# Four low halves back on GpSimd and three loads behind named pieces, in the first mixer of a two-layer block

## The chip, the cores and the metric

The kernel runs on one core of a Trainium2 chip. A core has a matrix engine (TensorE, "PE" in the profile; its weight loads are listed as PEld), a vector engine (VectorE, DVE), a scalar engine (ScalarE, ACT), GpSimd (POOL) and a queue that issues the loads (SyncE, SP). Each works through its own list of instructions in order and waits for the others by semaphores. SBUF is the on-chip memory, PSUM the banks that TensorE writes. The metric is the device time of one execution in microseconds (us); lower is better. Times quoted as "median" are over several executions; every row of the profile is from one profiled execution.

## The reference, cut to what matters

Two layers over 256 tokens of width 2048, all in float32. Layer 0 mixes by a convolution and by averages over windows ("pool"), layer 1 by a short gated convolution; each is followed by a gated feed-forward layer. Only the first mixer is touched by the change:

```python
def conv_pool_mixer(x, norm_g, w_in, conv_w, conv_b, ln_g, ln_b, w_pool, pool_scale, w_out):
    h = rms_norm(x, norm_g)
    u = h @ w_in                                   # 2048 -> 3 * 1024
    a = u[..., :D_CONV] * jax.nn.sigmoid(u[..., D_CONV:2 * D_CONV])
    a = causal_depthwise_conv(a, conv_w) + conv_b  # 31 taps
    a = jax.nn.silu(layer_norm(a, ln_g, ln_b))
    p = multiscale_pool(u[..., 2 * D_CONV:], w_pool, pool_scale)   # windows 2, 4, 8, 16, then 256 x 256 per group
    return jnp.concatenate([a, p], axis=-1) @ w_out

def reference(...):
    ...
            h = h + conv_pool_mixer(...)
        ...
        h = h + swiglu(rms_norm(h, ffn_norm[i]), w_gate[i], w_up[i], w_down[i])
    return rms_norm(h, final_norm)
```

## The kernel before, in words

**Weights and products.** Activations are kept with features on the 128 partitions and the 256 tokens along the row. All weights lie in one tensor (`wall`) in the order of their use, cut into blocks of 128 x 128. `fetch(u)` (L207) loads one unit of up to 16 blocks, 1024 KB, into one of four buffers named `w`; the first nine units are smaller and carry the first chunks of the input as well. A unit is used in pieces of 8 blocks (of 4 in the first units). For each piece, `prepare` (L222) calls `halves_of` (L213): ScalarE rounds the piece to the matrix engine's format (`hi`, L218), and another engine subtracts (`lo = w - hi`, L219). `hi` and `lo` have five buffers each, and some pieces use a spare pair. A block's product is three matmuls (L311 to L313): hi times the rounded activations, hi times their remainder, lo times the rounded activations. So TensorE needs a piece's low half before it can finish the first block of that piece. `advance` (L251) prepares up to four pieces ahead of the block in use in the first mixer, and fetches one unit beyond that.

**Who subtracts.** VectorE makes the low halves, except for the pieces whose first block number lies in `POOL_SPLIT` (72 to 519): these go to GpSimd. `relief` is a list to which each pool group adds one entry when it has been written out (L681); the next such piece that is prepared takes the entry and goes to VectorE. There are four pool groups, so four pieces go to VectorE: those that start at blocks 128, 224, 328 and 360.

**The first mixer's order on TensorE.** The first 64 blocks are four chunks side by side (two of the convolution, each with its gate), then come the two chunks of pool group 3 (64 to 95), and then the rest by `M0_ORDER`: a convolution chunk and its gate are 32 blocks, a pool group's two chunks 32, a group's own 256 x 256 matrix 4. The convolutions end at block 391, the groups 1 and 0 are 392 to 399, the projection of the pool half is 400 to 527, and the projection of the convolution half follows.

**What runs beside it.** `gated` multiplies a convolution chunk by its gate (VectorE L477, L633, L634). `tap` then convolves two chunks with 31 taps on VectorE, accumulating in PSUM (L536, L538), with half of the products made by ScalarE (L533) and added by VectorE (L540). `pooled` evicts a group's chunks on VectorE (L668), sums over the window in doubling steps on GpSimd (L674), corrects the first tokens (L676) and subtracts the input (L677); ScalarE rounds the result (L679) and VectorE writes its remainder (L680, two operands from SBUF). The layer norm's first part (`ln_mean`, `ln_center`) runs from VectorE, GpSimd and four matmuls of TensorE (L568); its last part (`ln_last`) starts with VectorE's L547 after the last tap, passes TensorE (L595, L587, L419) and ends with ScalarE's L624 and L626, from which the convolution half's projection reads.

**The input norm.** The square sum per token is taken from token rows: `square_rows(j)` (L495) loads 128 tokens by 2048 (1024 KB) into the one buffer `rows` and squares them on ScalarE (L498). From the two sums come the factors per token, spread to all partitions by a diagonal (VectorE L409, with the identity that lies at the end of `vec`) and a product (TensorE L419); VectorE copies the result (L461) and the first chunks can be evicted.

**What sets the order.** The context is opened with `schedule_with_timeline_sim=True`: the order of instructions on each engine is fixed when the program is built, from the order of the program text, its dependencies and an estimated timeline. `tc.issue_after(ins)` adds that what is issued inside stands behind `ins` on the same queue. `behind_weights(dst, src)` (L485) queues a load behind the latest `fetch` of the text so far (`state_pe["dma"]`).

Of the kernel before, what the change touches and what calls it, by code (L numbers as in the profile page):

```python
# [20 lines left out]
NC = D // P  # L21
# [101 lines left out]
def x_of(u):  # L123
    return X_CHUNKS[u] if u < len(X_CHUNKS) else 0
# [63 lines left out]
def block_kernel(ctx: ExitStack, tc: tile.TileContext, xT: bass.AP, xtok: bass.AP, vec: bass.AP, wall: bass.AP, out: bass.AP):  # L188
    nc = tc.nc
# [9 lines left out]
    banks = {}  # L199
    loaded, ready = {}, {}  # L200
    cursor = {"token": 0, "piece": 0, "P": 0, "S": 0}
    relief = []

    def new_acc(shape=(P, T), name="acc"):
        return banks["acc"].tile(list(shape), F32, name=name, tag="acc")

    def fetch(u):  # L207
        if u < len(UNITS) and u not in loaded:
            n, off = UNITS[u][3], UNIT_AT[u] * P * P
            loaded[u] = w = wst.tile([P, 16 * P], F32, name="w")  # L210
            state_pe["dma"] = nc.sync.dma_start(w[:, : n * P], wall[off : off + n * P * P].rearrange("(p f) -> p f", p=P)).ins

    def halves_of(src, at, n, engine, spare=False):  # L213
        if spare:
            hi, lo = (banks["spare"].tile([P, W_ROOM], F32R, name=x)[:, SPARE_AT : SPARE_AT + n] for x in ("hi", "lo"))
        else:
            hi, lo = (whl.tile([P, W_ROOM], F32R, name=x)[:, at : at + n] for x in ("hi", "lo"))
        state_pe["hi"] = nc.scalar.copy(hi, src).ins  # L218
        engine.tensor_tensor(out=lo, in0=src, in1=hi, op=ALU.subtract)  # L219
        return hi, lo  # L220

    def prepare(i):  # L222
        if i >= len(PIECES):
            return
        _, u, key, what = PIECES[i]
        if key in ready:
            return
        fetch(u)
        w = loaded[u]
        if key[0] == "P":  # L230
            o, n = what
            if x_of(u):
                for j in range((o - 2 * x_of(u)) // 4, (o - 2 * x_of(u) + n) // 4):
                    norm.scale(sum(X_CHUNKS[:u]) + j, w[:, j * T : (j + 1) * T])
            engine = nc.vector
            if key[1] in POOL_SPLIT:
                if relief:
                    relief.pop()
                else:
                    engine = nc.gpsimd  # L240
            ready[key] = halves_of(w[:, o * P : (o + n) * P], 0, n * P, engine, key[1] in SPARE and i % 6 == 5)
            return
        lo, n = ((0, 512), (1024, 1024), (0, 1024), (1024, 1024))[what]
        ready[key] = halves_of(w[:, lo : lo + n], S_SHIFT, n, nc.vector)
        if what == 0:
            nc.vector.tensor_tensor(out=w[:, :1024], in0=w[:, 512:1536], in1=w[:, :1024], op=ALU.subtract)
        if what == 1:
            nc.vector.tensor_tensor(out=w[:, 1024:1536], in0=w[:, 1024:1536], in1=w[:, :512], op=ALU.subtract)
            nc.vector.tensor_tensor(out=w[:, 1536:], in0=w[:, 1024:1536], in1=w[:, 1536:], op=ALU.subtract)
# [13 lines left out]
    def next_block():  # L263
        assert KINDS[cursor["token"]] == 0
        advance()
        b = cursor["P"]
        cursor["P"] = b + 1
        at = max(k[1] for k in ready if k[0] == "P" and k[1] <= b)
        hi, lo = ready[("P", at)]
        for k in [k for k in ready if k[0] == "P" and k[1] < at]:  # L270
            ready.pop(k)
        o = (b - at) * P
        return hi[:, o : o + P], lo[:, o : o + P]
# [22 lines left out]
    def tick():  # L296
        for name, q in queues.items():
            credit[name] = credit[name] + 1.0 if q else 0.0
            while q and credit[name] >= PACE[q[0][0]]:
                cost, step = q.popleft()  # L300
                credit[name] -= PACE[cost]
                step()
# [7 lines left out]
    def product(acc, hi, lo, x, first, last, part=False):  # L310
        nc.tensor.matmul(acc, hi, x[:, :T], start=first, stop=False, skip_group_check=part)  # L311
        nc.tensor.matmul(acc, hi, x[:, T:], start=False, stop=False, skip_group_check=part)  # L312
        state_pe["last"] = nc.tensor.matmul(acc, lo, x[:, :T], start=False, stop=last, skip_group_check=part).ins  # L313

    def matmul_chunks(xs, ks, n=1, behind=None, accs=None):


        accs = accs or [new_acc() for _ in range(n)]
        for i, k in enumerate(ks):
            first, last = i == 0, i == len(ks) - 1  # L320
            x = xs[k] if isinstance(xs, dict) else xs[:, k, :]
            for acc in accs:
                hi, lo = next_block()
                product(acc, hi, lo, x, first, last)
                tick()
            if behind is not None:
                behind(k)
        return accs
# [14 lines left out]
    v = const.tile([P, NVEC], F32, name="v")  # L343
# [138 lines left out]
    xs = norm.xs  # L482
    nc.sync.dma_start(v[:, :NC], vec[:, :NC])

    def behind_weights(dst, src):  # L485
        with tc.issue_after(state_pe["dma"]):
            nc.sync.dma_start(dst, src)

    def loads_behind(k):
        if k == 3:  # L490
            behind_weights(v[:, NC:], vec[:, NC:])
        if k == 4:
            square_rows(1)

    def square_rows(j):  # L495
        rows = x0_pool.tile([P, D + 64], F32, name="rows")[:, :D]
        behind_weights(rows, xtok[:, j, :])
        nc.scalar.activation(rows, rows, AF.Square, accum_out=rowsq[:, j : j + 1])  # L498

    x0 = ctx.enter_context(ExitStack())  # L500
    x0_pool = x0.enter_context(tc.tile_pool(name="x0", bufs=1))
    rowsq = const.tile([P, 2], F32, name="rowsq")
    for u in range(6):
        fetch(u)
    square_rows(0)
    every = range(NC)
    with tc.tile_pool(name="ps0", bufs=5, space=PSUM) as ps0, tc.tile_pool(name="m0", bufs=1) as m0, tc.tile_pool(name="ps_side", bufs=2, space=PSUM) as ps_side:
        phase[0] = m0, None, 2
# [120 lines left out]
        def gated(acc_v, acc_g, c):  # L629
# [7 lines left out]
            if c % 2:  # L637
                convolve(c - 1)

        first = matmul_chunks(xs, every, n=4, behind=loads_behind)  # L640
        rest = norm.rstd(rowsq, behind=True)
        for at in (0, NC // 2):
            behind_weights(h[:, at : at + NC // 2, :], xT[:, at : at + NC // 2, :])
# [15 lines left out]
        def pooled(g, accs=None):  # L659


            w = WINDOWS[g]
            xp = m0.tile([P, 2, pp + T], F32, name="xp", bufs=2)
            nc.gpsimd.memset(xp[:, :, :pp], 0.0)
            less = m0.tile([P, 2, T], F32, name="pm", bufs=2)
            for j in range(2):
                acc = accs[j] if accs else matmul_chunks(xs, every)[0]
                nc.vector.tensor_tensor(out=xp[:, j, pp:], in0=acc, in1=r, op=ALU.mult)  # L668
                nc.scalar.activation(less[:, j, :], xp[:, j, pp:], AF.Copy, scale=-float(w))
            cur, step = xp, 1  # L670
            while step < w:
                nxt = m0.tile([P, 2, pp + T], F32, name="sw", bufs=2)
                lo = pp - (w - 2 * step)
                nc.gpsimd.tensor_tensor(out=nxt[:, :, lo:], in0=cur[:, :, lo:], in1=cur[:, :, lo - step : pp + T - step], op=ALU.add)  # L674
                cur, step = nxt, 2 * step
            nc.gpsimd.tensor_tensor(out=cur[:, :, pp : pp + w - 1], in0=cur[:, :, pp : pp + w - 1], in1=corr[:, g, :, : w - 1], op=ALU.mult)  # L676
            nc.gpsimd.tensor_tensor(out=less, in0=cur[:, :, pp:], in1=less, op=ALU.add)  # L677
            dst = cat[:, 2 * g : 2 * g + 2, :]
            nc.scalar.activation(dst[:, :, :T], less, AF.Copy, scale=1.0 / w)  # L679
            nc.vector.scalar_tensor_tensor(out=dst[:, :, T:], in0=less, scalar=1.0 / w, in1=dst[:, :, :T], op0=ALU.mult, op1=ALU.subtract)  # L680
            relief.append(1)  # L681

        room = moving(x0_pool.tile([P, D + 64], F32R, name="room", tag="rows"), Y_AT, 4)
        mixed = {}
        for kind, i in M0_ORDER:
            if kind == "pool":
                pooled(i, early)
                early = None
                continue
            if kind == "group":  # L690
                for j in range(2):
                    (acc,) = matmul_chunks(cat, range(2 * i, 2 * i + 2))
                    mixed[2 * i + j] = xs[:, 2 * i + j, :] if i < 2 else room[:, 2 * i + j - 4, :]
                    split(mixed[2 * i + j], acc, col("pool_scale", 2 * i + j))
                continue
            (acc_v,) = matmul_chunks(xs, every)
            (acc_g,) = matmul_chunks(xs, every)
            gated(acc_v, acc_g, i)
# [315 lines left out]
```

## Time and profile before

| | us |
|---|---|
| median of 3 executions | 2008.69 (2006.31 to 2010.91) |
| the profiled execution | 2007.14 |
| its span, first to last instruction | 2004.9 |

| busy | us of the span | share |
|---|---|---|
| TensorE | 1984.6 | 99% |
| VectorE | 1706.8 | 85% |
| ScalarE | 1158.7 | 58% |
| GpSimd | 203.1 | 10% |

How to read the rows: in a timeline a row is start, duration, engine, line, operation, output tile <- input tiles, shapes and the number of merged instructions; a bracket at its end is the idle time before it and what ended it. A row of grouped instructions gives the count, then after the first bar the busy time (us) and the mean of one (ns), and after the second bar the idle time before them. A row of a stage begins with the stage's bounds and length, followed by the busy time and count of TensorE, its weight loads, VectorE, ScalarE and GpSimd, the granted clock of TensorE (1.00 is full), the share of DMA time, and GB/s. A row of one line's instructions gives the shortest, median and longest duration in ns, and the first and last start.

### The profile page before, as it was taken

How to read it: one execution, taken by the hardware profiler on the slowest of the kernel's cores; microseconds unless marked ns; L12 is line 12 of the kernel's file. 1: busy time of each engine (PE TensorE's matmuls, PEld its weight loads, DVE VectorE, ACT ScalarE, POOL GpSimd, SP SyncE). 2: the span in 40 equal slices, each digit the busy share in tenths (PEclk: the TensorE clock that was granted, in tenths of full speed). 3: DMA queues.
4: the chain of work that ended last, by engine and by line, in shares of the span. 5: the costliest groups of instructions: out<-in, count | busy, mean ns of one | idle time of the engine just before them, and what ended most of it. 6: DMA issues, size and time to landing. Idle time of an engine off the chain costs nothing.

```text
span 2004.9 us, 41548 instructions
## 1 busy us (share of the span) xinstructions
PE 1984.6 (99%) x17346; PEld 1981.3 (99%) x17346; DVE 1706.8 (85%) x2302; ACT 1158.7 (58%) x1527; POOL 203.1 (10%) x184
## 2 busy tenths in 40 slices
PE   9999999999999999999999999999999999999998
PEld 9999999999999999999999999999999999999997
DVE  6998888999988999989666666788999988999985
ACT  7788675655555555556444444565555555555554
POOL 3996200000000000002000001100000000000002
PEclk9999999999999999999999999999999999999999
DMA  9555445545555555546555555454554555555552
GB/s 362 189 190 211 148 171 208 202 185 207 206 196 205 190 210 199 203 191 229 189 193 198 199 190 191 167 211 171 208 210 190 210 211 209 200 201 190 190 228 88
DMA packets 55772, 398.27 MB, mean 199 GB/s; under 512 B 6304, under 2 KB 6560, under 8 KB 8352
## 3 DMA queue, kind: packets, MB, share of 16 engines
q1 hardware_dynamic: 55584, 395.61, 52.9%
q8 instruction: 136, 2.23, 0.4%
q14 instruction: 52, 0.43, 0.1%
HBM read 393.49 MB, written 2.10 MB: 197 GB/s over the span
## 4 chain that ended last, share of the span: by engine, by line
PE 92%; DVE 5%; ACT 1%; DMA 1%; issue 0%; DVEq 0%; SPq 0%; POOL 0%; ACTq 0%; POOLq 0%
PE acc L312 22%; PE acc L311 22%; PE acc L313 22%; PE s L796 8%; PE s L797 8%; PE s L795 8%; DVE side L538 2%; DVE side L540 1%; DVE lo L219 1%; PE acc L751 1%; DMA rows<-in_xtok 0%; PE s L311 0%; PE s L312 0%; PE s L313 0%; ACT hi L218 0%
## 5 line engine op out<-in xcount | busy, mean ns | idle before, releaser
L218 ACT CAST hi<-w 128x1024 fp32r<-128x1024 f32 (+1 forms) x933 | 922.4, 1004 | 742.9 <-PE acc L312 347.3
L219 DVE TENSOR_TENSOR lo<-w,hi 128x1024 fp32r<-128x1024 f32 (+1 forms) x881 | 1014.1, 1174 | 184.4 <-ACT hi L218 172.2
L311 PE MATMUL acc<-xs,hi 128*128 128x256 f32 x2416 | 663.0, 276 | 3.0 <-DVE gate L477 2.6
L312 PE MATMUL acc<-xs,hi 128*128 128x256 f32 x2416 | 662.4, 276 | 0.0
L313 PE MATMUL acc<-xs,lo 128*128 128x256 f32 x2416 | 660.1, 276 | 1.0 <-POOL lo L219 1.0
L311 PEld LDWEIGHTS acc<-xs,hi 128*128 128x128 f32 x2416 | 452.9, 188 | 4.1 <-ACT prod L533 1.7
L312 PEld LDWEIGHTS acc<-xs,hi 128*128 128x128 f32 x2416 | 452.6, 188 | 0.0
L313 PEld LDWEIGHTS acc<-xs,lo 128*128 128x128 f32 x2416 | 450.8, 188 | 1.5 <-POOL lo L219 1.2
L312 PE MATMUL acc<-y,hi 128*128 128x256 f32 x1408 | 387.7, 276 | 0.0
L311 PE MATMUL acc<-y,hi 128*128 128x256 f32 x1408 | 387.6, 276 | 0.0
L313 PE MATMUL acc<-y,lo 128*128 128x256 f32 x1408 | 383.5, 276 | 0.0
L312 PEld LDWEIGHTS acc<-y,hi 128*128 128x128 f32 x1408 | 264.4, 188 | 0.0
L311 PEld LDWEIGHTS acc<-y,hi 128*128 128x128 f32 x1408 | 264.2, 188 | 0.0
L313 PEld LDWEIGHTS acc<-y,lo 128*128 128x128 f32 x1408 | 262.2, 188 | 0.0
L795 PE MATMUL s<-hi,sf 128*128 128x256 f32 x768 | 210.9, 277 | 0.0
L796 PE MATMUL s<-hi,sf 128*128 128x256 f32 x768 | 210.0, 275 | 0.0
L450 POOL TENSOR_TENSOR sumsq<-sumsq,sq 128x256 f32<-128x256 f32 x56 | 53.2, 951 | 1526.7 <-ACT sq L448 1526.3
L797 PE MATMUL s<-lo,sf 128*128 128x256 f32 x768 | 206.5, 276 | 0.0
L797 PE MATMUL s<-lo,xs 128*128 128x256 f32 x576 | 159.0, 276 | 0.0
L795 PE MATMUL s<-hi,xs 128*128 128x256 f32 x576 | 159.0, 276 | 0.0
L796 PE MATMUL s<-hi,xs 128*128 128x256 f32 x576 | 158.8, 276 | 0.0
L795 PEld LDWEIGHTS s<-hi,sf 128*128 128x128 f32 x768 | 144.3, 188 | 0.0
(193 smaller groups left out, 2665.1 us busy)
## 6 DMA issues: line engine op xcount, KB each, us to landing
w<-in_wall SPq DMA_DIRECT2D x365, 1024.0 KB, 4.9
w<-in_wall SPq DMA_DIRECT2D x7, 768.0 KB, 7.3
rows<-in_xtok SPq DMA_DIRECT2D x2, 1024.0 KB, 8.6
h<-in_xT SPq DMA_DIRECT2D x2, 1024.0 KB, 11.8
out<-res SPq DMA_DIRECT2D x2, 512.0 KB, 2.7
w<-in_wall SPq DMA_DIRECT2D x2, 384.0 KB, 4.1
out<-res SPq DMA_DIRECT2D x2, 384.0 KB, 2.7
v<-in_vec SPq DMA_DIRECT2D x1, 260.0 KB, 7.6
```

The lines of the kernel that those rows point to most:

```text
L218: state_pe["hi"] = nc.scalar.copy(hi, src).ins
L219: engine.tensor_tensor(out=lo, in0=src, in1=hi, op=ALU.subtract)
L311: nc.tensor.matmul(acc, hi, x[:, :T], start=first, stop=False, skip_group_check=part)
L312: nc.tensor.matmul(acc, hi, x[:, T:], start=False, stop=False, skip_group_check=part)
L313: state_pe["last"] = nc.tensor.matmul(acc, lo, x[:, :T], start=False, stop=last, skip_group_check=part).ins
L450: nc.gpsimd.tensor_tensor(out=self.sums[0], in0=self.sums[0], in1=sq, op=ALU.add)
L538: nc.vector.scalar_tensor_tensor(out=dst, in0=src, scalar=wt, in1=dst, op0=ALU.mult, op1=ALU.add)
L540: nc.vector.tensor_tensor(out=side, in0=side, in1=prods.pop((c, k)), op=ALU.add)
L751: nc.tensor.transpose(bank[:, c, t * P : (t + 1) * P], part[:, c * P : (c + 1) * P], identity)
L795: nc.tensor.matmul(acc, xh, hi, start=first, stop=False, skip_group_check=True)
L796: nc.tensor.matmul(acc, xl, hi, start=False, stop=False, skip_group_check=True)
L797: nc.tensor.matmul(acc, xh, lo, start=False, stop=last, skip_group_check=True)
```

## The change

Two things are done. First, `relief` is removed: every piece in `POOL_SPLIT` has its low half made by GpSimd, the four at blocks 128, 224, 328 and 360 among them. Second, three loads are attached to pieces of the weights by number: `fetch` looks up its unit in `load_behind` and runs what it finds right behind that unit's load. The first token rows stand behind unit 5 as before. The rest of `vec` (the vectors, with the identity) stands behind unit 6; before, it was issued at the end of the fourth input chunk of the first products. The second token rows stand behind unit 8; before, they were issued at the end of the fifth input chunk, behind the latest load of that moment (unit 7).

```diff
     cursor = {"token": 0, "piece": 0, "P": 0, "S": 0}
-    relief = []
...
+    load_behind = {}
 
     def fetch(u):
         if u < len(UNITS) and u not in loaded:
...
+            if u in load_behind:
+                load_behind[u]()
...
             if key[1] in POOL_SPLIT:
-                if relief:
-                    relief.pop()
-                else:
-                    engine = nc.gpsimd
+                engine = nc.gpsimd
...
-    def loads_behind(k):
-        if k == 3:
-            behind_weights(v[:, NC:], vec[:, NC:])
-        if k == 4:
-            square_rows(1)
-
...
+    load_behind[5] = partial(square_rows, 0)
+    load_behind[6] = lambda: behind_weights(v[:, NC:], vec[:, NC:])
+    load_behind[8] = partial(square_rows, 1)
     for u in range(6):
         fetch(u)
-    square_rows(0)
...
-        first = matmul_chunks(xs, every, n=4, behind=loads_behind)
+        first = matmul_chunks(xs, every, n=4)
...
-            relief.append(1)
```

## The prediction

> **What bounds the kernel now.** I read the page first, then the busy time by stages, TensorE's waits, and the timelines of VectorE and GpSimd.
>
> ```profile
> span 2004.9 us, 41548 instructions
> PE 1984.6 (99%) x17346; PEld 1981.3 (99%) x17346; DVE 1706.8 (85%) x2302; ACT 1158.7 (58%) x1527; POOL 203.1 (10%) x184
> ...
> 52.00:138.00 86.00, 85.80 (x756) 85.80 (x757) 82.20 (x138) 65.25 (x119) 81.50 (x46) 1.00 0.55 197
> 138.00:158.00 20.00, 15.62 (x128) 14.96 (x127) 17.06 (x32) 18.72 (x35) 20.00 (x11) 1.00 0.53 194
> ```
>
> TensorE is busy 1984.6 of 2004.9 us, so a change outside its work can win back only its 20 us of waits. The stage rows (busy time of TensorE, its weight load, VectorE, ScalarE, GpSimd, each with its count) show that the first mixer is different from the average: GpSimd, 10% busy over the span, is busy 81.50 of 86.00 us there and 20.00 of 20.00 in the next stage. VectorE is nearly as full. TensorE waits little before 138 us, then 4.4 us in 20. Its waits, one row each, in time order (the bracket holds the wait and its releaser):
>
> ```profile
> 52.20 0.39 PE L313 MATMUL acc<-xs,lo 128*128 128x256 f32 x1 [0.98 <-POOL lo L219]
> 140.54 0.36 PE L311 MATMUL acc<-xs,hi 128*128 128x256 f32 x1 [1.57 <-DVE gate L477]
> 147.73 1.13 PE L568 MATMUL st<-total,ones 128*128 128x256 f32 x4 [2.25 <-DVE total L552]
> 149.76 0.28 PE L313 MATMUL acc<-cat,lo 128*128 128x256 f32 x1
> 152.30 0.38 PE L311 MATMUL acc<-cat,hi 128*128 128x256 f32 x1 [0.56 <-DVE gate L477]
> 204.68 1.33 PE L311 MATMUL acc<-cat,hi 128*128 128x256 f32 x5 [2.67 <-ACT cat L626]
> ```
>
> Three of the first four waits end on VectorE. Why VectorE is late is seen in its low halves; the first four rows are those that the change moves (blocks 128, 224, 328 and 360), the fifth is one run after GpSimd has finished:
>
> ```profile
> 48.30 1.59 DVE L219 TENSOR_TENSOR lo<-w,hi 128x1024 fp32r<-128x1024 f32 x1
> 75.75 8.40 DVE L219 TENSOR_TENSOR lo<-w,hi 128x1024 fp32r<-128x1024 f32 x1
> 115.73 3.77 DVE L219 TENSOR_TENSOR lo<-w,hi 128x1024 fp32r<-128x1024 f32 x1
> 128.50 2.17 DVE L219 TENSOR_TENSOR lo<-w,hi 128x1024 fp32r<-128x1024 f32 x1
> 186.25 1.21 DVE L219 TENSOR_TENSOR lo<-w,hi 128x1024 fp32r<-128x1024 f32 x1
> ...
> 47.72 1.08 POOL L674 TENSOR_TENSOR sw<-xp 128x540 f32<-128x540 f32 x1
> 48.77 3.38 POOL L219 TENSOR_TENSOR lo<-w,hi 128x1024 fp32r<-128x1024 f32 x1
> 53.19 7.22 POOL L219 TENSOR_TENSOR lo<-w,hi 128x1024 fp32r<-128x1024 f32 x3
> 77.21 4.81 POOL L219 TENSOR_TENSOR lo<-w,hi 128x1024 fp32r<-128x1024 f32 x2
> 81.97 1.10 POOL L677 TENSOR_TENSOR pm<-sw,pm 128x512 f32<-128x512 f32 x1
> ```
>
> The same subtraction takes 1.21 us alone and up to 8.40 us here. The 8.40 us row ends at 84.15, which is 1.08 us after GpSimd's L677 ends at 83.07: VectorE did its work only when GpSimd stopped. The reverse is at 48.77, where GpSimd's subtraction takes 3.38 us instead of 7.22 / 3 = 2.41, while VectorE's runs. So the two shut each other out when both read two operands from SBUF. The four rows hold VectorE for 15.93 us.
>
> **The change, part by part.** *What VectorE loses:* 15.93 us of work and blocking ahead of the waits at 140.54, 147.73 and 152.30. Beside that, 0.97 us of GpSimd's 3.38 goes, and with it the 0.98 us wait at 52.20: this subtraction (block 120) then ends at 48.80 + 2.41 = 51.2, where TensorE stood. Gross gain 0.98 + 1.57 + 2.25 + 0.56 = 5.36 us, and what is late next has to be looked for on GpSimd.
>
> *What GpSimd gets:* four subtractions, 4 x 2.41 = 9.64 us, in its most crowded stretch. Its own rows (count, busy and mean, idle time and releaser), the first for 48.75 to 147 us, the others for 45 to 185:
>
> ```profile
> L219 POOL TENSOR_TENSOR lo<-w,hi 128x1024 fp32r<-128x1024 f32 x32 | 79.2, 2498 | 0.2 <-ACT hi L218 0.2
> ...
> L674 POOL TENSOR_TENSOR sw<-sw 128x512 f32<-128x512 f32 (+3 forms) x6 | 6.6, 1102 | 0.0
> L677 POOL TENSOR_TENSOR pm<-sw,pm 128x512 f32<-128x512 f32 x4 | 4.4, 1102 | 0.0
> L674 POOL TENSOR_TENSOR sw<-xp 128x540 f32<-128x540 f32 (+3 forms) x4 | 4.2, 1058 | 4.3 <-DVE xp L668 4.3
> ...
> L676 POOL TENSOR_TENSOR sw<-sw,corr 128x30 f32<-128x30 f32 (+3 forms) x4 | 1.9, 471 | 0.0
> ...
> 129.54 1.20 POOL L676 TENSOR_TENSOR sw<-sw,corr 128x6 f32<-128x6 f32 x1
> ...
> L313 PE MATMUL acc<-xs,lo x203: 275/275/275, 59.8 to 129.9; 128*128 128x256 f32 x102
> L313 PE MATMUL acc<-cat,lo x4: 275/275/275, 98.2 to 99.3; 128*128 128x256 f32 x4
> ```
>
> Take the piece of block 392, the first group after the last convolution chunk, whose low half TensorE now reads at 149.76. From 48.80 GpSimd has done 31 subtractions up to it (the 32nd of the first row is the next piece); with the change it has 35: 35 x 2.41 = 84.4 us. The pool's own operations in that stretch are 6.6 + 4.4 + 4.2 + 1.9 = 17.1, less the L674 of 47.72 (1.08) that lies before it, less one L677 (1.1) that comes after it, less about 1.0 in L676, of which the one at 129.54 was itself shut out (1.20 us, where the mean of the other three is 0.2): 13.9 us. The 4.3 us in which GpSimd waited for VectorE's L668 are gone too, since VectorE is early. End: 48.80 + 84.4 + 13.9 = 147.1. Three of VectorE's L680 also read two SBUF operands and can hold GpSimd for at most their own 0.68 us each, 0 to 2.0; I take 1.2 from the middle: **148.3**.
>
> TensorE without any wait: 203 + 4 low products in 59.8 to 129.9 are 70.1 / 206 = 0.340 us a block. From 51.22 (52.20 less 0.98) 272 blocks are 92.5 us, with 0.8 for L568's four products 144.5. So TensorE would be at block 392 at 144.5 and GpSimd delivers at 148.3: GpSimd takes VectorE's place as bound, and 3.8 us of the gain is spent on waits for low halves. Against 149.76 this leaves 1.5 us. The wait of 0.56 at 152.30 goes as well: 2.0 us.
>
> *The layer norm behind it* keeps part. Its rows, with what GpSimd does beside the first of VectorE's:
>
> ```profile
> 144.87 12.29 POOL L219 TENSOR_TENSOR lo<-w,hi 128x1024 fp32r<-128x1024 f32 x5
> 147.91 2.22 DVE L680 SCALAR_TENSOR_TENSOR cat<-pm,cat 128x512 fp32r<-128x512 f32 x1 [0.23 <-ACT cat L679]
> 151.84 0.41 DVE L477 TENSOR_TENSOR gate<-acc,rstd 128x256 f32<-128x256 f32 x1
> 189.44 0.68 DVE L547 TENSOR_TENSOR conv<-side,mean 128x512 f32<-128x512 f32 x1
> 191.32 1.02 PE L595 MATMUL side<-conv,parts 128*128 128x256 f32 x4
> ```
>
> The last gate (151.84) stands behind the last L680 on VectorE, and L680 behind GpSimd's last pool operation, which GpSimd's fuller queue makes no earlier. From that gate the last 31 taps run to L547, whose end at 190.12 TensorE uses at 191.32: 1.2 us to spare. If the gate stays where it is, only 1.2 of the 2.0 us pass; if it comes earlier with VectorE, all. I take **1.5 us**. The 2.67 us at 204.68 stay: it waits for a chain that starts from TensorE's own later product.
>
> *The loads.* The first rows load keeps its place. The vectors follow unit 6 in either text. The second rows load may not go before unit 8; the queue already has it behind unit 9 (the load at 17.81). The first row is a stage's, its last number GB/s:
>
> ```profile
> 20.00:40.00 20.00, 18.89 (x162) 18.31 (x161) 12.63 (x29) 17.14 (x27) 10.32 (x5) 1.00 1.01 421
> ...
> 17.81 0.33 SPq L211 DMA_DIRECT2D w<-in_wall  x1
> 19.19 0.33 SPq L487 DMA_DIRECT2D rows<-in_xtok  x1
> ...
> 28.57 1.93 ACT L498 ACTIVATE rows<-rows 128x2048 f32<-128x2048 f32 x1 [0.45 <-DMA rows<-in_xtok]
> 32.18 0.48 DVE L409 TENSOR_TENSOR diag<-v,st 128x128 f32<-128x128 f32 x2
> 35.11 0.59 PE L419 MATMUL st<-diag,ones 128*128 128x256 f32 x2
> 36.77 0.35 PE L311 MATMUL acc<-xs,hi 128*128 128x256 f32 x1 [1.07 <-DVE gate L477]
> ```
>
> It waits at 19.19 for the rows buffer, not for its place. The diagonal is ready at 32.66 and used at 35.11, by TensorE's order: 2.4 us of cover. So 0 us. Bounds: if this order of products moved up, at most the 1.07 us wait at 36.77 would go (gain 1.1); if the load slipped behind two more units of 1024 KB, each takes 2.5 us at the 421 GB/s of the first row, and 5.0 less the cover of 2.4 would be lost (2.6).
>
> Sum on the profiled execution: 2007.14 us (span 2004.9 and 2.2 around it) less 1.5 is 2005.6. The profiled run lies 1.55 below the median of 2008.69, so the median goes to **2007.2**. Below about 4 us (0.2%) no measurement of this kernel tells a difference: the likeliest outcome is no visible change.
>
> A rule against the change stands in the Trainium skill, "GPSIMD Engine Reference", section 4.1: elementwise work with two inputs belongs on VectorE, as GpSimd is about twice as slow. By the rows it is 2.41 to 1.21, so the trace agrees for a VectorE left alone, and disagrees here, where VectorE's four took 15.93 us against 9.64. The skill's "SBUF — State Buffer", section "Who interferes with whom", says that of two such instructions the one that issues second is blocked until the first finishes. By that rule no VectorE wait would exceed one GpSimd operation, about 2.4 us; the 8.40 us row goes against it, for it sat through several. With the rule rival A below would cost little more than 2 us and end as the forecast does.
>
> **The rivals.** *A: L680 starves (slower).* The last L680 (147.91) took 2.22 us, since it got in between two subtractions. With four more in its queue GpSimd has fewer pauses, and L680 can be passed over as the row of 75.75 was: 8.40 - 1.21 = 7.2 us. The last group's products need its result, and the last gate and the taps stand behind it. Then L680 ends about 7 us later than the 150.1 of now, and TensorE, which passed at 152.30, stands until 157 to 158 and loses 5 to 6: 2008.7 + 5.5 = **2014.2**. It decides from a wait of some 4 us on. Against it: beside 147.91 stood a run of five subtractions (144.87) and L680 got in.
>
> *B: the pool operations move up (faster).* Without the row of 75.75 VectorE evicts the pool's sums up to 7.2 us earlier, so GpSimd's order may have the last pool operation several subtractions earlier. Then the layer norm starts early and its 2.67 us wait shrinks too: 5.36 + 2.67 less GpSimd's 2.6 (144.5 to 147.1) is 5.4: **2003.3**. Against it: the order is fixed when the program is built, and nothing shows that it was made with VectorE's blocking in it.
>
> *C: the change doesn't keep the loads in place*: the second rows load slips by two units and costs its 2.6 us on top: 2009.8, still within 0.2%.
>
> **How the numbers follow.** Forecast (GpSimd takes over as bound, about 1.5 us) 0.46; A 0.20; B 0.30; C 0.04. By the bound of 0.2% the forecast and C are the same, apart from a little on each side of A and B: faster 0.30, same 0.49, slower 0.21. The range runs from B's lower part, 2001.5 (all waits of the first sum gone and most of 2.67), to A's price, 2014.5, and leaves about 1 in 10 at each end.
>
> **What would show it.** Right: no L219 on VectorE between 38 and 180; GpSimd without a pause from 48 on, its stretch to block 392 ending near 148; TensorE waiting in many small pieces for low halves on GpSimd between 52 and 150, 3 to 4 us in all, and no longer for L477 and L552. A would show as an L680 above 5 us, B as the last L677 well before 143. Wrong at the root would be a GpSimd with pauses: then its rate is not the bound, and the gain is larger.

## The result, and the profile after

The changed kernel takes **2027.58 us** (median, 2026.35 to 2028.09) against 2008.69: 1.0093 of the time before, interval 1.0079 to 1.0107. It is slower by 19 us, outside the range given. The profiled execution took 2026.43 us. Its page, and four of its stages (bounds, length, busy time and count of TensorE, its weight loads, VectorE, ScalarE and GpSimd, TensorE's granted clock, DMA share, GB/s):

```profile
span 2024.7 us, 41558 instructions
PE 1986.5 (98%) x17346; PEld 1982.9 (98%) x17346; DVE 1709.0 (84%) x2298; ACT 1161.3 (57%) x1527; POOL 209.3 (10%) x188
...
80.00:100.00 20.00, 18.04 (x160) 17.84 (x158) 18.44 (x29) 15.16 (x26) 20.00 (x13) 1.00 0.59 208
100.00:120.00 20.00, 9.33 (x64) 9.34 (x65) 18.63 (x18) 6.70 (x13) 13.19 (x7) 0.66 0.46 159
140.00:160.00 20.00, 17.38 (x135) 16.83 (x134) 12.56 (x24) 13.06 (x23) 13.76 (x9) 0.91 0.42 155
160.00:180.00 20.00, 13.17 (x97) 12.56 (x96) 12.55 (x23) 15.66 (x34) 15.46 (x11) 0.83 0.30 106
```

TensorE's idle time in the span was 2004.9 - 1984.6 = 20.3 us and is 2024.7 - 1986.5 = 38.2: 17.9 of the 19.8 us by which the span grew are waits, and the other 1.9 are a longer busy time for the same 17346 products. The loss is in one place above all. Between 100 and 120 TensorE runs 64 products where a full stage has 179 (60 to 80, before and after), while VectorE looks busy (18.63 of 20.00). TensorE's waits there and later, from its timeline:

```profile
110.67 0.80 PE L312 MATMUL acc<-cat,hi 128*128 128x256 f32 x2 [12.63 <-DVE cat L676]
149.15 2.08 PE L564 MATMUL st<-total,ones 128*128 128x256 f32 x4 [2.62 <-DVE total L548]
165.79 0.50 PE L311 MATMUL acc<-cat,hi 128*128 128x256 f32 x2 [1.60 <-ACT cat L675]
172.97 0.80 PE L311 MATMUL acc<-cat,hi 128*128 128x256 f32 x2 [5.01 <-ACT cat L675]
208.62 0.67 PE L419 MATMUL st<-diag,ones 128*128 128x256 f32 x2 [2.73 <-DVE diag L608]
```

The first group's own product (group 3) waits 12.63 us for the remainder of that group, which VectorE writes with L676 (L680 of the kernel before). The waits at 165.79 and 172.97, 6.6 us, are for the rounded sums of two later groups. Those at 149.15 and 208.62 are about as long as two of the kernel before (2.25 and 2.67). What VectorE, ScalarE and GpSimd did meanwhile, from their timelines:

```profile
95.79 14.82 DVE L676 SCALAR_TENSOR_TENSOR cat<-pm,cat 128x512 fp32r<-128x512 f32 x1
...
111.90 0.42 ACT L627 ACTIVATE gate<-gate 128x256 f32<-128x256 f32 x1 [13.34 <-DVE gate L477]
...
93.98 1.11 POOL L673 TENSOR_TENSOR pm<-sw,pm 128x512 f32<-128x512 f32 x1
95.03 2.46 POOL L222 TENSOR_TENSOR lo<-w,hi 128x1024 fp32r<-128x1024 f32 x1
97.40 0.16 POOL L660 MEMSET xp<- 128x30 f32 x1
97.47 6.98 POOL L222 TENSOR_TENSOR lo<-w,hi 128x1024 fp32r<-128x1024 f32 x3
104.38 1.08 POOL L670 TENSOR_TENSOR sw<-sw 128x520 f32<-128x520 f32 x1
105.39 4.67 POOL L222 TENSOR_TENSOR lo<-w,hi 128x1024 fp32r<-128x1024 f32 x2
116.30 2.44 POOL L222 TENSOR_TENSOR lo<-w,hi 128x1024 fp32r<-128x1024 f32 x1 [6.24 <-ACT hi L221]
```

Read the ends. L676 ends at 95.79 + 14.82 = 110.61. GpSimd's unbroken run ends at 105.39 + 4.67 = 110.06 and then it is idle for 6.24 us. An operation that takes 0.68 us for another group is reported as 14.82: it stood shut out until GpSimd had nothing left. Of VectorE's 18.63 us "busy" between 100 and 120, 10.6 are this. Its next gate waits behind it, ScalarE waits 13.34 us for that gate, and with ScalarE stopped no more halves are rounded: only then does GpSimd run dry, and VectorE gets in. So the queue of ready subtractions, not one of them, sets the length of the block.

There is a second difference. L673, which completes group 3's sum, starts at 93.98; in the kernel before, the same operation (L677) started at 81.97. TensorE is at the group at 110.67 - 12.63 = 98.04 in both cases, near enough, so 12 us of slack had gone before the block began.

### The profile page after: what moved, and what is told of

Read it like the earlier page. It is cut to its first block, busy times and chain, and to the rows that moved or that the text cites. A ratio compares the mean times of both kernels' runs of the same rounds, so it can differ in the third digit from the quotient of the medians.

```text
span 2024.7 us, 41558 instructions
## 1 busy us (share of the span) xinstructions
PE 1986.5 (98%) x17346; PEld 1982.9 (98%) x17346; DVE 1709.0 (84%) x2298; ACT 1161.3 (57%) x1527; POOL 209.3 (10%) x188
## 4 chain that ended last, share of the span: by engine, by line
PE 96%; DVE 2%; ACT 1%; DMA 1%; issue 0%; POOL 0%; SPq 0%; DVEq 0%; POOLq 0%; ACTq 0%
PE acc L311 24%; PE acc L313 24%; PE acc L312 24%; PE s L792 8%; PE s L791 8%; PE s L790 8%; DVE cat L676 1%; PE acc L746 1%; DMA rows<-in_xtok 0%; PE s L313 0%; PE s L311 0%; PE s L312 0%; ACT hi L221 0%; ACT prod L529 0%; DMA w<-in_wall 0%
## 5 line engine op out<-in xcount | busy, mean ns | idle before, releaser
L222 DVE TENSOR_TENSOR lo<-w,hi 128x1024 fp32r<-128x1024 f32 (+1 forms) x877 | 997.2, 1160 | 185.7 <-ACT hi L221 173.1
```

## The experiments

Two theories were set against each other. **Starvation:** VectorE's operations with two SBUF operands are shut out by GpSimd's unbroken runs. **Overload and order:** GpSimd has too much to do, and the pool's operations come late in its queue. "The kernel before" is timed beside each group of runs; the ratio is to it, and is not the quotient of two medians.

| run | median us | ratio, 95% interval |
|---|---|---|
| e1_loads | 2008.32 | 1.0007 (0.9994 to 1.0020) |
| e2_relief | 2027.07 | 1.0084 (1.0053 to 1.0116) |
| e3_psum | 2035.75 | 1.0135 (1.0114 to 1.0156) |
| e4_pause | 2025.95 | 1.0086 (1.0065 to 1.0107) |
| e5_st3 | 2018.66 | 1.0058 (1.0041 to 1.0075) |
| e8_relief_two | 2024.19 | 1.0086 (1.0069 to 1.0104) |
| e9_relief_late | 2025.80 | 1.0090 (1.0072 to 1.0108) |
| e10_dense | 2024.06 | 1.0084 (1.0063 to 1.0105) |
| e12_dense_st | 2005.57 | 0.9986 (0.9978 to 0.9995) |
| e13_st_all | 2008.74 | 1.0003 (0.9994 to 1.0013) |
| e14_pause256 | 2028.60 | 1.0101 (1.0088 to 1.0115) |
| e15_relief_dense_st | 2010.19 | 1.0008 (0.9999 to 1.0017) |

### Which half of the change: the loads, or the low halves

Two runs take one half each: the loads moved with `relief` kept, and `relief` removed with the loads left.

```diff
 # e2_relief, from the kernel before
...
             if key[1] in POOL_SPLIT:
-                if relief:
-                    relief.pop()
-                else:
-                    engine = nc.gpsimd
+                engine = nc.gpsimd
...
```

> The kernel before with the loads alone moved (vectors behind unit 6, second token rows behind unit 8); four low halves still go to VectorE. Starvation theory (the changed kernel is slower because VectorE's last operation of pool group 3, with two SBUF operands, is shut out by GpSimd's unbroken run for 14.8 us): the loads cost nothing, 2008.7 within 3 us. Rival (the loads shift the order at the start): above 2013.

> The kernel before with only the relief list removed, loads where they were. Starvation theory and overload theory (GpSimd has too much work) alike: the whole loss, 2027 within 3 us. If the loads matter: between 2009 and 2023.

The loads cost nothing (2008.32), and the low halves are the whole loss (2027.07, with L676's 14.8 us in its trace as well). The loads' run shows something else. Two of the four low halves in its VectorE timeline:

```profile
76.70 2.39 DVE L223 TENSOR_TENSOR lo<-w,hi 128x1024 fp32r<-128x1024 f32 x1
...
111.10 8.44 DVE L223 TENSOR_TENSOR lo<-w,hi 128x1024 fp32r<-128x1024 f32 x1
```

In the kernel before, the second and third of the four took 8.40 and 3.77 us. Here they take 2.39 and 8.44, and the total is the same within the interval: which operation is shut out, and for how long, turns on small shifts.

### Taking the second SBUF operand away

In e3 ScalarE copies each group's result to one of the accumulator banks in PSUM, and VectorE reads it there.

```diff
 # e3_psum, from the changed kernel
+            bank = new_acc((P, 2, T))
+            nc.scalar.copy(bank, less)
-            nc.vector.scalar_tensor_tensor(out=dst[:, :, T:], in0=less, ...)
+            nc.vector.scalar_tensor_tensor(out=dst[:, :, T:], in0=bank, ...)
```

> The changed kernel, but ScalarE copies each pool group's result to a PSUM bank and VectorE reads it there, so that the group's last operation has one SBUF operand. Four more ScalarE copies of about 0.6 us; the values are the same. Starvation theory: group 3's last operation takes about 0.7 us instead of 14.8, the 12.6 us wait of TensorE before that group goes, 2027.6 - 12.6 = 2015 or less (the clock that is lowered after the wait returns too). Overload theory: GpSimd's work is unchanged, at most 3 us faster, 2024 or more.

The operation itself is as starvation has it, but the time is the worst of all. Its row (shortest, median and longest duration in ns) and the longest wait of TensorE:

```profile
L678 DVE SCALAR_TENSOR_TENSOR cat<-acc,cat x4: 681/688/692, 62.6 to 160.5; 128x512 fp32r<-128x512 f32 x4
...
155.90 2.07 PE L564 MATMUL st<-total,ones 128*128 128x256 f32 x4 [15.52 <-DVE total L548]
```

All four take 0.69 us. But the bank is one of the five that TensorE accumulates in, and the order on all engines came out different, with a wait of 15.52 us in another place. The time would fit overload's 2024 or more, but with another order on every engine it speaks for neither theory. The same was tried for group 3 alone, in the bank of the token sums (`ps_st`), which is free at that time; GpSimd's order stays that of the changed kernel.

```diff
 # e5_st3, from the changed kernel
+            if g == 3:
+                bank = ps_st.tile([P, 2, T], F32, name="st", tag="st")
+                nc.scalar.copy(bank, less)
-            nc.vector.scalar_tensor_tensor(out=dst[:, :, T:], in0=less, ...)
+            nc.vector.scalar_tensor_tensor(out=dst[:, :, T:], in0=bank if g == 3 else less, ...)
```

> The changed kernel, with pool group 3's result alone copied by ScalarE to the bank of the token sums, which is free there, and read from it by VectorE; no accumulator bank is taken and GpSimd's order is that of the changed kernel. Starvation theory: the group's last operation takes 0.7 us and not 14.8, TensorE's 12.6 us wait before the group goes: 2027 - 12.6 = 2014.5, or less by the clock that it lowers. Order theory (the pool's operations stand behind more low halves, and what counts is when group 3's sum is ready): the sum is ready at 95 as before and TensorE is there at 98, so the wait goes here too; the later waits (7 us) stay by either. Overload theory: GpSimd's rate bounds, 2022 or more.

```profile
97.70 0.69 DVE L679 SCALAR_TENSOR_TENSOR cat<-st,cat 128x512 fp32r<-128x512 f32 x1
139.24 5.84 DVE L679 SCALAR_TENSOR_TENSOR cat<-pm,cat 128x512 fp32r<-128x512 f32 x1
...
165.59 0.79 PE L311 MATMUL acc<-cat,hi 128*128 128x256 f32 x2 [6.79 <-ACT cat L675]
```

Group 3's operation takes 0.69 us instead of 14.82, TensorE doesn't wait for it, and the time falls to 2018.66, 9 us less. The 2014.5 that starvation expected was missed by 4. One reason is in the rows: the next group's operation, which still reads two SBUF operands, is now shut out for 5.84 - 0.68 = 5.2 us. Then all four groups were read from that bank:

> The changed kernel with all four groups' results read from the token sums' bank, GpSimd's order free. Starvation theory: no operation of VectorE above 1.3 us in the stage; about 5 us less than with group 3 alone (2018.7), 2013 to 2015. Order theory: the last groups' results still come when TensorE is already there, so 5 to 9 us of waits on the groups stay, and the time stays above 2012.

```profile
L678 DVE SCALAR_TENSOR_TENSOR cat<-st,cat x4: 681/688/692, 97.1 to 158.1; 128x512 fp32r<-128x512 f32 x4
...
136.65 0.80 PE L311 MATMUL acc<-cat,hi 128*128 128x256 f32 x2 [4.21 <-ACT cat L675]
157.26 0.79 PE L311 MATMUL acc<-cat,hi 128*128 128x256 f32 x2 [3.74 <-ACT cat L675]
```

2008.74: nearly all of the 19 us is gone, more than either theory expected (2013 to 2015, and above 2012). GpSimd has the same work as in the changed kernel, and up to its operation at 149.25 there it does it in the same order, so overload is not the loss. What the order theory says is there too (7.95 us of waits for groups that come late), but it only makes up for the waits that the change did remove: up to 215 us the waits listed for TensorE are 11.3 us, and 10.3 in the kernel before.

### Giving GpSimd a pause

A tiny GpSimd operation that needs what VectorE's last operation of the group writes makes GpSimd stop there; the operands stay as they are. In e4 each group has one, put by the program's builder wherever it fell; in e14 only group 3 has one, and the low halves from block 256 on are ordered behind it.

```diff
 # e14_pause256, from the changed kernel (e4_pause: for every g, without the order)
+            if g == 3:
+                gap = m0.tile([P, 2, 1], F32R, name="gap", bufs=1)
+                gaps[256] = nc.gpsimd.tensor_tensor(out=gap, in0=less[:, :, :1], in1=dst[:, :, T : T + 1], op=ALU.subtract).ins
...
+        with tc.issue_after(behind) if behind is not None else nullcontext():
+            engine.tensor_tensor(out=lo, in0=src, in1=hi, op=ALU.subtract)
```

> The changed kernel with one tiny GpSimd operation behind each pool group that reads an element of what VectorE's last operation of the group writes, so GpSimd has to pause there until VectorE is through. Starvation theory: that operation takes at most one GpSimd subtraction and its own time, 2.4 + 0.7 = 3.1 us, wherever the pause stands early enough; TensorE's 12.6 us wait shrinks to under 4, 2016 to 2020. If the blocking ended with each single GpSimd operation anyway, the pauses change nothing: 2027.

> The changed kernel with the operands as they are; GpSimd pauses once: the low halves from block 256 on stand behind a tiny GpSimd operation that needs VectorE's last operation of group 3. Starvation theory: that operation takes under 3.2 us instead of 14.8 with the same operands in the same place, TensorE's 12.6 us wait falls under 3, GpSimd loses 2 to 3 us by the pause: 2015 to 2020. If the 14.8 us had another cause than GpSimd's unbroken run (its operands, a bank, the tile), it stays above 10 us and the time at 2027.

In e4 the pause of group 3 fell late, so the time is 2025.95 and not the 2016 to 2020 of the starvation theory. But it did let VectorE in: GpSimd stops for 0.63 us, VectorE's operation ends at 108.58, and GpSimd goes on at once with a subtraction that was ready.

```profile
96.07 12.51 DVE L676 SCALAR_TENSOR_TENSOR cat<-pm,cat 128x512 fp32r<-128x512 f32 x1
...
108.66 0.20 POOL L678 TENSOR_TENSOR gap<-pm,cat 128x2 fp32r<-128x2 f32 x1 [0.63 <-DVE cat L676]
108.81 2.38 POOL L222 TENSOR_TENSOR lo<-w,hi 128x1024 fp32r<-128x1024 f32 x1
```

In e14 group 3's operation is short, though not by the pause. VectorE's rows for groups 3 and 2, GpSimd's around them, and TensorE's two waits:

```profile
95.74 0.98 DVE L678 SCALAR_TENSOR_TENSOR cat<-pm,cat 128x512 fp32r<-128x512 f32 x1
121.77 12.79 DVE L678 SCALAR_TENSOR_TENSOR cat<-pm,cat 128x512 fp32r<-128x512 f32 x1
...
95.12 2.51 POOL L672 TENSOR_TENSOR sw<-sw 128x520 f32<-128x520 f32 x2
97.59 0.19 POOL L681 TENSOR_TENSOR gap<-pm,cat 128x2 fp32r<-128x2 f32 x1
...
132.96 1.05 POOL L672 TENSOR_TENSOR sw<-sw 128x512 f32<-128x512 f32 x1
136.75 2.38 POOL L224 TENSOR_TENSOR lo<-w,hi 128x1024 fp32r<-128x1024 f32 x1 [2.74 <-ACT hi L222]
...
134.62 0.80 PE L314 MATMUL acc<-cat,hi 128*128 128x256 f32 x2 [10.00 <-DVE cat L678]
171.38 0.80 PE L313 MATMUL acc<-cat,hi 128*128 128x256 f32 x2 [12.42 <-ACT cat L677]
```

Group 3's operation starts at the same time as in the changed kernel, has the same operands, and takes 0.98 us. So the 14.82 come from what GpSimd runs beside it and not from the operation itself. But VectorE is through at 96.72, before GpSimd comes to the tiny operation at 97.59, and no idle time is listed before that. What the edit had changed by then is GpSimd's order. With the later low halves held back, two doubling steps of group 2 stand at 95.12, where the changed kernel runs a subtraction, and VectorE got in between them: the two take 2.51 us together, where such a step alone takes 1.1. So e14 doesn't test the pause; only e4 does.

The time did not fall either (2028.60, where 2015 to 2020 was expected): group 2, which has no pause, is shut out for 12.79 us, until GpSimd's run ends at 132.96 + 1.05 = 134.01, and TensorE waits there instead. With one operation freed, the next of the four is held. The wait of 12.42 us is for ScalarE to round a later group's sum, with no operation of VectorE held beside it.

### Half of the low halves, and GpSimd's order

Two runs let only two of the four go to VectorE: the first two (blocks 128 and 224), or the last two (328 and 360).

```diff
 # e8_relief_two, from the kernel before (e9_relief_late: if g < 2)
-            relief.append(1)
+            if g >= 2:
+                relief.append(1)
```

> The kernel before, but only the first two of the four low halves (blocks 128 and 224) go to VectorE; the other two stay on GpSimd. Starvation theory: up to group 3 all is as before, so the 12.6 us wait doesn't arise; what is lost is at most the later waits (7 us): 2008 to 2016. Overload theory: half of the loss, 2018.

> The kernel before, but only the last two of the four (blocks 328 and 360) go to VectorE; the first two stay on GpSimd. Starvation theory: GpSimd's run around group 3 is that of the changed kernel, so the 12.6 us wait is there: 2020 or more. Overload theory: half of the loss, 2018.

The two longest rows of e8's L680:

```profile
120.84 7.52 DVE L680 SCALAR_TENSOR_TENSOR cat<-pm,cat 128x512 fp32r<-128x512 f32 x1
157.12 5.52 DVE L680 SCALAR_TENSOR_TENSOR cat<-pm,cat 128x512 fp32r<-128x512 f32 x1 [1.11 <-ACT cat L679]
```

In e9 the 12.59 us wait at group 3 is there, as expected. In e8 it is not, also as expected, but the time was not 2008 to 2016: in its stretch with all halves on GpSimd two later groups are shut out (7.52 and 5.52 us). Overload's 2018 came out in neither run. Half of the relief saves next to nothing (2024.19 and 2025.80 against 2027.58): in both runs long blocks are left.

In e10 GpSimd's order alone was changed: each low half stands behind one further operation of the group, so that a group's sum is ready early (near 68 and not 95 for group 3).

```diff
 # e10_dense, from the changed kernel; steps collects the pool's operations
+        with tc.issue_after(steps.pop(0)) if engine is nc.gpsimd and steps else nullcontext():
+            engine.tensor_tensor(out=lo, in0=src, in1=hi, op=ALU.subtract)
```

> The changed kernel with GpSimd's order alone altered: each low half that is prepared after a pool group stands behind one further operation of that group, so a group has one low half between its operations and not three or four. The work is the same. Order theory (the loss is that a group's result comes late, next to the moment when TensorE needs it): group results come 10 to 25 us earlier, a blocked VectorE operation no longer holds TensorE at the group, and the 7 us of later waits go: 2005 to 2012. Starvation theory alone (each long GpSimd run blocks VectorE's last operation of a group, wherever it stands): VectorE still loses over 10 us at it, and TensorE waits elsewhere for VectorE: 2015 or more. Overload theory: 2024 or more.

```profile
69.97 12.74 DVE L678 SCALAR_TENSOR_TENSOR cat<-pm,cat 128x512 fp32r<-128x512 f32 x1
...
147.22 13.46 DVE L678 SCALAR_TENSOR_TENSOR cat<-pm,cat 128x512 fp32r<-128x512 f32 x1
...
89.01 0.58 PE L313 MATMUL acc<-xs,hi 128*128 128x256 f32 x1 [10.33 <-ACT hi L222]
161.35 2.07 PE L566 MATMUL st<-total,ones 128*128 128x256 f32 x4 [8.22 <-DVE total L550]
```

The order theory alone would have given 2005 to 2012; it gave 2024.06. (Overload's 2024 or more fits this run too; e13 speaks against it.) The first block starts 26 us earlier, far from the group's product, and is paid all the same: with VectorE shut out, ScalarE stops behind it for 12.43 us, and TensorE waits 10.33 us for a rounded piece. The second, for a later group, is followed by a wait of 8.22 us for VectorE's sum. Early or late, the shut-out is paid.

### Both cures, and the change under them

e12 has e10's order and e13's operand; e15 is the same with the four low halves on VectorE, so the two differ by the change under study.

> The changed kernel with both cures: GpSimd's pool operations closer together (one low half between two of them) and all four groups' results copied by ScalarE to the token sums' bank, so that VectorE's last operation of a group has one SBUF operand. All low halves of the range stay on GpSimd. If starvation and the late order together are the loss: the waits of 12.6, 10 and 8 us are all gone, what is left is GpSimd's rate, 3 to 4 us of waits for low halves, 2003 to 2009. If GpSimd's load is a loss of its own: 2014 or more.

> The kernel before with the two cures of the run of 2005.6 (closer pool operations, all four groups read from the token sums' bank) while the four low halves still go to VectorE. It differs from that run by the change under study alone. Starvation theory: the four low halves, which have two SBUF operands, are the only operations left on VectorE that can be shut out; at least one of them is, for 5 us or more, and this kernel is slower than 2005.6 by 1 to 8 us, so that the change would be a gain once nothing else of VectorE's can be shut out. Rival (with the cures GpSimd is the bound, and four subtractions less on it are a relief): 2003 to 2005.

From e12, the two longest of its six waits for low halves; then from e15 the worst of the four low halves and the wait that follows:

```profile
64.22 0.39 PE L315 MATMUL acc<-xs,lo 128*128 128x256 f32 x1 [0.58 <-POOL lo L224]
...
105.46 0.39 PE L315 MATMUL acc<-cat,lo 128*128 128x256 f32 x1 [1.49 <-POOL lo L224]
```

```profile
111.81 10.88 DVE L221 TENSOR_TENSOR lo<-w,hi 128x1024 fp32r<-128x1024 f32 x1
...
149.53 2.07 PE L570 MATMUL st<-total,ones 128*128 128x256 f32 x4 [2.97 <-DVE total L554]
```

With both cures and all low halves on GpSimd the kernel takes 2005.57 us, 0.9986 of the time before (0.9978 to 0.9995): faster than both kernels, if little. With the four low halves on VectorE it takes 2010.19. One of them is shut out for 10.88 us, VectorE then works without idle time until 148.40, and its sum comes 2.97 us late. Of the 5.1 us between the two spans (2009.2 and 2004.1) 2.8 are a longer busy time of TensorE (1986.7 and 1983.9), so not all of the gap can be read from the waits. Between these two kernels the change is worth 2010.19 - 2005.57 = 4.6 us, where the four pool operations can't be shut out; it costs 19 us where they can.

## Why the prediction was wrong, point by point

**The forecast's case failed at one step:** "Three of VectorE's L680 also read two SBUF operands and can hold GpSimd for at most their own 0.68 us each". That priced one side of the shut-out only, what VectorE takes from GpSimd. The other side, what GpSimd's run takes from VectorE, was 14.8 us at the first L680 alone. The row that priced it was in the text, 8.40 us at 75.75. The sign given for a root error, a GpSimd with pauses, did come (6.24 us at 110.06), but with a loss and not a larger gain: GpSimd paused because VectorE's block had stopped ScalarE.

**Rival A had the mechanism, with too little chance and the wrong size.** It placed the block at the last group and priced it at 7.2 us by that row. It came at the first group and is not a fixed price: it lasts as long as GpSimd finds ready work. Giving GpSimd the four subtractions closed its pauses: its first run without idle time was 45.33 to 83.07 before and is 45.38 to 110.06 now. The sign given for A, an L680 above 5 us, came. The chance of 0.20 rested on the one L680 that "got in" at 147.91, and the longer rows spoke against it.

**That GpSimd's order stays** was wrong as well. Both the forecast and rival B took GpSimd's order as before or better. With four subtractions more, the builder put four between two pool operations of group 3 where there had been three, and that group's sum came 12 us later (93.98 against 81.97). This used up the slack in front of the group's product. It made the loss fall on that wait. It was not the cause of the whole: in e10 the sums come early and the time stays at 2024.06, and e13 takes 2008.74 with the order of the changed kernel.

**GpSimd's rate was sized right, but it bound elsewhere.** In e12, where none of VectorE's four pool operations is held, GpSimd is busy all the time from 48 to 160, and the last of the 35 subtractions that the forecast counted ends at 146.6, against 147.1. TensorE is at that block's product only at 150.5 and doesn't wait there. Its waits for low halves are six, 3.1 us in all, between 51 and 106. That they come near the 3.8 us of the forecast is luck. Waits that VectorE ended (L477, L552) were to vanish; in e12 one of 0.9 us for L477 and none for the total is left.

**The loads** cost nothing, as forecast, with the queue's order unchanged.

**One operation or a whole run.** The Trainium skill's "SBUF — State Buffer", section "Summary: rules for kernel authors", has the second of two such instructions blocked until the first finishes. The runs show more: 14.82 us in the changed kernel outlasts the subtraction it met, five more and one pool operation of GpSimd. The advice of the Trainium skill in the same row, to schedule the one that is off the critical path, is tested by no run here; e13 takes an operand away instead.

**Which engine should subtract.** The Trainium skill's "GPSIMD Engine Reference", section 4.1, would leave such subtractions on VectorE. By e12 and e15 they are better on GpSimd here, by 4.6 us, though each is twice as long (2.41 to 1.21 us).

**What stays open:** why an operation of VectorE sometimes gets in between two of GpSimd's and sometimes not. In the traces it got in either at the end of the GpSimd operation that it met (2.22 us at 147.91 before, 2.39 us in e1, 0.98 us in e14), or, once passed over, only at GpSimd's next pause (every row above 3 us that is shown). What decides at that first end, the runs don't show.

## What to carry to other kernels

Where VectorE and GpSimd share a stage, list the operations of VectorE with two SBUF operands: each can be held for as long as GpSimd's queue has ready work, early or late in the stage. Filling GpSimd's pauses takes away the places where VectorE gets in, so a move that balances the busy times can lose more than it shifts. Take the second SBUF operand away first (here a 0.6 us copy to PSUM by ScalarE), then move the work. Here that alone gave back the loss and no gain (e13, 1.0003); the small gain of e12 came with the closer order of GpSimd's operations as well.

## What the runs showed of the hardware that was not expected

A shut-out that outlasts GpSimd's current operation ends with GpSimd's pause: 14.82 us in the changed kernel, 12.79 in e14, 12.74 and 13.46 in e10, for an operation that takes 0.68 to 0.69 us from PSUM. The first two end 0.55 us after GpSimd's last operation. The profile books such time as VectorE's busy time, so a stage with 18.63 of 20.00 us busy can be one in which VectorE stands still for 10.6. And a long wait of TensorE costs more than itself: in the stage 100 to 120, with the wait of 12.63 us, the granted clock is 0.66, and 64 products take 9.33 us, 0.146 each against 20.00 / 179 = 0.112 in a full stage.
